# A streaming cross-entropy kernel: 7168 columns instead of 8192 per transfer, and a last chunk of 1024 columns

## Chip, cores, metric

One NeuronCore of a Trainium2 chip. The metric is the device time of one execution in microseconds (us); the runs of a kernel agree within about 0.3%. The span of a profile is about 2 us shorter than the device time of the same run.

## The reference

```python
def reference(pred, target):          # both float32, 8192 x 8192
    eps = 1e-7
    pred = np.clip(pred, eps, 1 - eps)
    return -(target * np.log(pred) + (1 - target) * np.log(1 - pred))
```

The targets are 0 or 1, so the kernel computes -ln|pred + target - 1|: one logarithm per element.

## The kernel before

It views each matrix as 64 chunks of 128 partitions x 8192 columns. A chunk is one contiguous piece of 4 MiB, so neighbouring partitions' rows lie 32 KiB apart. Four slots of a ring hold chunks in flight; target is converted to bf16 by its transfer. Each chunk takes `clip` (DVE), `front` (subtract-add on DVE, then Abs and Ln on ACT), `back` (multiply by -1, DVE) and a store.

```python
W = 8192
SLOTS = 4
# ... (rings, slot)
    def load(k):
        queue = nc.sync if k == 0 else nc.gpsimd
        queue.dma_start(out=slot(ring_p, k), in_=pred_c[k])
        nc.gpsimd.dma_start(out=slot(ring_t, k), in_=target_c[k])

    def store(k, off=0, w=W):
        queue = nc.sync if k >= n - 2 else nc.gpsimd
        queue.dma_start(out=out_c[k, :, off : off + w], in_=slot(ring_p, k, off, w))
# ... (clip, front, back; the first loads; clip(0), front(0))
        for k in range(1, n - 1):
            clip(k)
            front(k)
            back(k - 1)
            store(k - 1)
            if k >= 2 and k - 2 + SLOTS < n:
                load(k - 2 + SLOTS)
        clip(n - 1)
        back(n - 2)
        store(n - 2)
        # ... the last chunk in quarters, with two half stores
```

## Time and profile before

| | before |
|---|---|
| device time, first three runs | 1868.99 us (1868.84 to 1870.61) |
| busiest engine | DVE, 60% of the span |
| DMA | full in all 40 slices, 431 GB/s of HBM traffic |
| period of the loop | 29.05 us per chunk |
| transfers | 193 |

Read it from the bytes: 805.31 MB move in any version.

### The profile page before, as it was taken

To read this page: it belongs to the slowest core of one execution; us is meant where nothing else is said; L and a number is where in the kernel's file an instruction comes from. 1 tells how busy PE (TensorE), PEld (TensorE's weight loads), DVE (VectorE), ACT (ScalarE), POOL (GpSimd) and SP (SyncE) were. 2 spreads that over 40 slices of the span, in tenths; PEclk is the share of its full clock that TensorE was granted. 3 is DMA by queue.
4 is the path that set the end of the run, shared out by engine and by line. 5 is a ranking of instruction groups with operands and counts; after the bars stand their busy time and mean duration, and the time that the engine had idled before them with its cause. 6 is when DMAs were issued, how large, how long until landed. Compare 5 with 4: busy or idle time off the path is not lost.

```text
span 1867.5 us, 759 instructions
## 1 busy us (share of the span) xinstructions
DVE 1117.6 (60%) x199; ACT 902.4 (48%) x136; POOL 110.6 (6%) x193
## 2 busy tenths in 40 slices
DVE  4846564656656656566565665656656566566664
ACT  3643635546355364553644535445354463544635
POOL 0210000000000000000000000000000000000000
DMA  9999999999999999999999999999999999999999
GB/s 326 337 378 350 352 376 344 377 352 351 381 345 374 358 344 386 343 371 362 344 388 341 366 368 344 386 344 360 370 344 384 348 355 375 345 378 355 348 381 344
DMA packets 27797, 671.14 MB, mean 359 GB/s; under 512 B 3088, under 2 KB 3088, under 8 KB 3088
## 3 DMA queue, kind: packets, MB, share of 16 engines
q0 software_dynamic: 27216, 658.52, 98.9%
q1 hardware_dynamic: 576, 12.58, 1.6%
q14 instruction: 5, 0.04, 0.0%
HBM read 536.87 MB, written 268.44 MB: 431 GB/s over the span
## 4 chain that ended last, share of the span: by engine, by line
issue 87%; DMA 6%; POOL 5%; DVE 1%; ACT 1%; POOLq 0%; DVEq 0%; PEldq 0%
DMA ring_t<-in_target_dram 4%; DMA out_dram<-ring_p 2%; POOL ring_t L59 2%; POOL out_dram L63 2%; POOL ring_p L58 1%; DVE ring_p L73 1%; ACT ring_p L77 0%; ACT ring_p L76 0%; DVE ring_p L81 0%; POOLq L58 0%; DVEq L73 0%; PEldq L138 0%; POOLq L63 0%
## 5 line engine op out<-in xcount | busy, mean ns | idle before, releaser
L76 ACT ACTIVATE ring_p<-ring_p 128x8192 f32<-128x8192 f32 (+1 forms) x67 | 450.6, 6725 | 949.5 <-DVE ring_p L73 949.5
L73 DVE SCALAR_TENSOR_TENSOR ring_p<-ring_t,ring_p 128x8192 f32<-128x8192 bf16 (+1 forms) x67 | 556.6, 8309 | 326.0 <-DMA ring_t<-in_target_dram 326.0
L67 DVE TENSOR_SCALAR ring_p<-ring_p 128x8192 f32<-128x8192 f32 x64 | 283.3, 4426 | 406.6 <-DMA ring_p<-in_pred_dram 406.6
L77 ACT ACTIVATE ring_p<-ring_p 128x8192 f32<-128x8192 f32 (+1 forms) x67 | 450.6, 6725 | 2.1
L81 DVE TENSOR_SCALAR ring_p<-ring_p 128x8192 f32<-128x8192 f32 (+1 forms) x67 | 283.3, 4228 | 5.0 <-ACT ring_p L77 5.0
L63 POOL DMA_DIRECT2D out_dram<-ring_p x62 | 40.8, 659 | 1691.8 <-DVE ring_p L81 1661.8
L58 POOL DMA_DIRECT2D ring_p<-in_pred_dram x63 | 36.1, 574 | 18.7 <-DMA out_dram<-ring_p 18.4
L59 POOL DMA_DIRECT2D ring_t<-in_target_dram x64 | 35.3, 552 | 0.8 <-PEq L138 0.8
L87 ACT ACT_TABLE_LOAD x1 | 1.3, 1283 | 0.7 <-PEq L127 0.7
L86 DVE MEMSET warm<- 1x8 f32 x1 | 0.1, 65 | 0.8 <-PEq L127 0.8
L87 ACT ACTIVATE warm<-warm 1x8 f32<-1x8 f32 x1 | 0.2, 208 | 0.0
L127 POOL MEMSET const-float32-0.0<- 128x1 f32 x1 | 0.1, 98 | 0.2 <-issue 0.2
L127 POOL MEMSET const-bfloat16-1.0<- 128x1 bf16 x1 | 0.1, 101 | 0.0
L127 POOL MEMSET const-float32-1.0<- 128x1 f32 x1 | 0.1, 98 | 0.0
L127 POOL MEMSET const-uint8-127<- 128x1 uint8 x1 | 0.1, 98 | 0.0
## 6 DMA issues: line engine op xcount, KB each, us to landing
ring_p<-in_pred_dram POOLq DMA_DIRECT2D x63, 4096.0 KB, 34.5
out_dram<-ring_p POOLq DMA_DIRECT2D x62, 4096.0 KB, 25.3
ring_t<-in_target_dram POOLq DMA_DIRECT2D x64, 2048.0 KB, 43.7
ring_p<-in_pred_dram SPq DMA_DIRECT2D x1, 4096.0 KB, 19.5
out_dram<-ring_p SPq DMA_DIRECT2D x1, 4096.0 KB, 20.2
out_dram<-ring_p SPq DMA_DIRECT2D x2, 2048.0 KB, 11.6
```

The costliest lines, as they stand in the source:

```text
L58: queue.dma_start(out=slot(ring_p, k), in_=pred_c[k])
L59: nc.gpsimd.dma_start(out=slot(ring_t, k), in_=target_c[k])
L63: queue.dma_start(out=out_c[k, :, off : off + w], in_=slot(ring_p, k, off, w))
L67: nc.vector.tensor_scalar(out=p, in0=p, scalar1=EPS, scalar2=1 - EPS, op0=Alu.max, op1=Alu.min)
L73: nc.vector.scalar_tensor_tensor(out=p, in0=t, scalar=1.0, in1=p, op0=Alu.subtract, op1=Alu.add)
L76: nc.scalar.activation(out=p, in_=p, func=Act.Abs)
L77: nc.scalar.activation(out=p, in_=p, func=Act.Ln)
L81: nc.vector.tensor_scalar(out=p, in0=p, scalar1=-1.0, scalar2=None, op0=Alu.mult)
L86: nc.vector.memset(warm, 1.0)
L87: nc.scalar.activation(out=warm, in_=warm, func=Act.Ln)
L127: nc = _bacc.Bacc("TRN2", target_bir_lowering=False, num_devices=1)
```

## The change

The intent: a row pitch that is an odd number of 4 KiB (28 KiB instead of 32), and a tail in which only a small chunk comes last, behind two full stores, in place of a last chunk cut in quarters.

```diff
-W = 8192
+WIDE = 7 * 1024
 SLOTS = 4
+
+def plan(total):
+    n, last = divmod(total, WIDE)
+    assert 0 < last < WIDE
+    return [WIDE] * n + [last]
 ... (views and ring slots follow the widths)
-        clip(0)
-        front(0)
-        for k in range(1, n - 1):
+        for k in range(n):
             clip(k)
+            if k == n - 1:
+                back(k - 1)
+                store(k - 1)
             front(k)
-            back(k - 1)
-            store(k - 1)
+            if 0 < k < n - 1:
+                back(k - 1)
+                store(k - 1)
             if k >= 2 and k - 2 + SLOTS < n:
                 load(k - 2 + SLOTS)
-        clip(n - 1)
-        back(n - 2)
-        store(n - 2)
-        ... (quarters of the last chunk)
+        back(n - 1)
+        store(n - 1)
```

More of the change, by code (lines that the diff above doesn't have):

```diff
@@ L38, with chunk, slot @@
     R, C = pred.shape
-    n = R * C // (P * W)
-    assert n * P * W == R * C and n > SLOTS
-    def chunks(ap):
-        return ap.rearrange("r c -> (r c)").rearrange("(k p w) -> k p w", p=P, w=W)
-    pred_c, target_c, out_c = chunks(pred), chunks(target), chunks(out)
+    widths = plan(R * C // P)
+    n = len(widths)
+    cols = [sum(widths[:k]) for k in range(n)]
+    def chunk(ap, k):
+        flat = ap.rearrange("r c -> (r c)")
+        return flat[cols[k] * P : (cols[k] + widths[k]) * P].rearrange("(p w) -> p w", p=P)
     pool = ctx.enter_context(tc.tile_pool(name="rings", bufs=1))
-    ring_p = pool.tile([P, SLOTS * W], fp32, name="ring_p", tag="ring_p")
-    ring_t = pool.tile([P, SLOTS * W], bf16, name="ring_t", tag="ring_t")
+    ring_p = pool.tile([P, SLOTS * WIDE], fp32, name="ring_p", tag="ring_p")
+    ring_t = pool.tile([P, SLOTS * WIDE], bf16, name="ring_t", tag="ring_t")
     warm = pool.tile([1, 8], fp32, name="warm", tag="warm")
-    def slot(ring, k, off=0, w=W):
-        c = k % SLOTS * W + off
+    def slot(ring, k, off=0, w=None):
+        w = w or widths[k]
+        c = k % SLOTS * WIDE + off
         return ring[:, c : c + w]
@@ L57, in load, with store, clip @@
         queue = nc.sync if k == 0 else nc.gpsimd
-        queue.dma_start(out=slot(ring_p, k), in_=pred_c[k])
-        nc.gpsimd.dma_start(out=slot(ring_t, k), in_=target_c[k])
-    def store(k, off=0, w=W):
+        queue.dma_start(out=slot(ring_p, k), in_=chunk(pred, k))
+        nc.gpsimd.dma_start(out=slot(ring_t, k), in_=chunk(target, k))
+    def store(k, off=0, w=None):
+        w = w or widths[k]
         queue = nc.sync if k >= n - 2 else nc.gpsimd
-        queue.dma_start(out=out_c[k, :, off : off + w], in_=slot(ring_p, k, off, w))
-    def clip(k, off=0, w=W):
+        queue.dma_start(out=chunk(out, k)[:, off : off + w], in_=slot(ring_p, k, off, w))
+    def clip(k, off=0, w=None):
         p = slot(ring_p, k, off, w)
@@ L69, in clip, with front @@
         )
-    def front(k, off=0, w=W):
+    def front(k, off=0, w=None):
         p, t = slot(ring_p, k, off, w), slot(ring_t, k, off, w)
@@ L77, in front, with back @@
         nc.scalar.activation(out=p, in_=p, func=Act.Ln)
-    def back(k, off=0, w=W):
+    def back(k, off=0, w=None):
         p = slot(ring_p, k, off, w)
@@ L87 @@
         nc.scalar.activation(out=warm, in_=warm, func=Act.Ln)
-        clip(0)
-        front(0)
-        for k in range(1, n - 1):
+        for k in range(n):
             clip(k)
+            if k == n - 1:
+                back(k - 1)
+                store(k - 1)
             front(k)
-            back(k - 1)
-            store(k - 1)
+            if 0 < k < n - 1:
+                back(k - 1)
+                store(k - 1)
             if k >= 2 and k - 2 + SLOTS < n:
                 load(k - 2 + SLOTS)
-        clip(n - 1)
-        back(n - 2)
-        store(n - 2)
-        q = W // 4
-        front(n - 1, 0, q)
-        front(n - 1, q, q)
-        front(n - 1, 2 * q, q)
-        back(n - 1, 0, q)
-        back(n - 1, q, q)
-        store(n - 1, 0, 2 * q)
-        front(n - 1, 3 * q, q)
-        back(n - 1, 2 * q, q)
-        back(n - 1, 3 * q, q)
-        store(n - 1, 2 * q, 2 * q)
+        back(n - 1)
+        store(n - 1)
 _INS = ['pred', 'target']
```

## The prediction

> **What bounds the kernel now.** I read the page first: the busy table, the slices, the queue table and the HBM line. Then I read the issues with their landings, the waits, the groups by shape, the chain of waits in order of time, and last the timeline and the windows of the final 60 us.
>
> From the page:
>
> ```profile
> DVE 1117.6 (60%) x199; ACT 902.4 (48%) x136; POOL 110.6 (6%) x193
> DMA  9999999999999999999999999999999999999999
> ...
> q0 software_dynamic: 27216, 658.52, 98.9%
> ...
> HBM read 536.87 MB, written 268.44 MB: 431 GB/s over the span
> ```
>
> No engine is busy more than 60% of the span, while the DMA row is full in all 40 slices. The traffic is 536.87 + 268.44 = 805.31 MB, and the diff does not change it: each element of pred and target is still read once and each result written once. At 431 GB/s over the whole span the kernel moves data nearly as fast as it ever will.
>
> The issues with their landings give the unit cost:
>
> ```profile
> ring_p<-in_pred_dram POOLq DMA_DIRECT2D x63, 4096.0 KB, 34.5
> out_dram<-ring_p POOLq DMA_DIRECT2D x62, 4096.0 KB, 25.3
> ring_t<-in_target_dram POOLq DMA_DIRECT2D x64, 2048.0 KB, 43.7
> ```
>
> Per chunk the POOL queue gets a store, a pred load and a target load, one behind the other. They land 9.2 us apart and are issued 0.53 us apart, so each takes about 9.7 us. The target load reads 4 MiB of HBM although it writes only 2 MiB, because it converts to bf16. So the HBM side counts.
>
> The chain of waits in order of time shows the period of the loop (start, length, what):
>
> ```profile
> 135.42 27.61 issue
> 164.64 27.90 issue
> 194.15 28.24 issue
> 224.00 28.17 issue
> ...
> 428.98 27.49 issue
> 458.08 27.43 issue
> ...
> 1765.14 27.39 issue
> ```
>
> "Issue" here is POOL with nothing to do until the next store is ready. From 428.98 to 1765.14 there are 46 periods: 29.05 us each, and 12.583 MB per period is 433.2 GB/s. From 135.42 to 428.98 there are 10 periods of 29.36 us, so the early part lost about 3.1 us.
>
> The timeline of the end (start, length, engine):
>
> ```profile
> 1808.26 8.69 DVE L73 SCALAR_TENSOR_TENSOR ring_p<-ring_t,ring_p 128x8192 f32<-128x8192 bf16 x1 [5.29 <-DMA ring_t<-in_target_dram]
> 1816.87 4.42 DVE L81 TENSOR_SCALAR ring_p<-ring_p 128x8192 f32<-128x8192 f32 x1
> 1816.99 7.03 ACT L76 ACTIVATE ring_p<-ring_p 128x8192 f32<-128x8192 f32 x1 [14.95 <-DVE ring_p L73]
> 1821.59 0.54 POOL L63 DMA_DIRECT2D out_dram<-ring_p  x1 [27.45 <-DVE ring_p L81]
> 1824.05 7.03 ACT L77 ACTIVATE ring_p<-ring_p 128x8192 f32<-128x8192 f32 x1
> ...
> 1836.40 19.96 SPq L63 DMA_DIRECT2D out_dram<-ring_p  x3
> ```
>
> and the window of its stores:
>
> ```profile
> 1837.00:1856.00 19.00, 13.71 (x8) 14.95 (x8) 0.00 (x0) 1.00 0.99 426
> ```
>
> After the last target load has landed (1837.2) only stores remain, and the DMA share is still 0.99: the tail runs without a hole. Check: when the target of the chunk before the last lands, at 1808.26, six DMAs are left. 6 x 9.68 = 58.1 gives 1866.4, and the last data packet in the trace ends at 1866.0.
>
> **What the Trainium skill says.** (1) "DMA: Bandwidth & Descriptors", section "Where 436 GB/s comes from": 16 ports x 32 B x 850 MHz = 435.2 GB/s. The steady loop's 433.2 agrees and leaves 0.5%. (2) "HBM Reference", section "Specifications (TRN2)": a core's share is about 358 GB/s, but a core alone gets about 425. The trace shows 431, so this is the case of a core alone. (3) The DMA page, section "Latency and other measured facts": row pitches of large powers of two slow a copy, and 4 KiB of padding restored it. The pitches tabulated are 512 KiB and more; here it is 32 KiB and the steady loop is at full rate, so the trace shows no such loss outside perhaps the early 3.1 us. (4) Same page, "Specifications": first byte about 1 us after a GpSimd-issued DMA and 0.6 us after a Sync one. Here SP issued at 0.74 and the first packet started at 1.75: 1.0 us.
>
> **The change, part by part.** The diff changes the shape of the transfers: 64 chunks of 8192 columns become 73 of 7168 and one of 1024 (524288 = 73 x 7168 + 1024). I call them k = 0 to 73; s, p, t are store, pred load, target load.
>
> 1. *Steady loop.* 28.91 us of each 29.05 are 12.583 MB at 435.2 GB/s, so a DMA costs 0.045 us beyond its bytes. A wide DMA is 3.670 MB: 8.43 + 0.045 = 8.48 us. A small one is 0.524 MB: 1.25 us. There were 193 DMAs and there will be 222. Cost: 29 x 0.045 = **+1.3 us**.
>
> 2. *Does the queue stay fed?* From the landing of t(k), the DVE does 8.69 + 4.42 us before s(k-1) and the next loads are issued: 13.33 us (1808.26 to 1821.59). Three DMAs, 29.05 us, are queued then, so 15.7 us remain. After: the groups by shape have two widths, 8192 and 2048, so I interpolate.
>
> ```profile
> L73 DVE SCALAR_TENSOR_TENSOR ring_p<-ring_t,ring_p 128x8192 f32<-128x8192 bf16 x63 | 547.6, 8692 | 325.0 <-DMA ring_t<-in_target_dram 325.0
> L81 DVE TENSOR_SCALAR ring_p<-ring_p 128x8192 f32<-128x8192 f32 x63 | 278.4, 4419 | 0.0
> ...
> L73 DVE SCALAR_TENSOR_TENSOR ring_p<-ring_t,ring_p 128x2048 f32<-128x2048 bf16 x4 | 9.0, 2285 | 1.0 <-DMA ring_t<-in_target_dram 1.0
> ...
> L81 DVE TENSOR_SCALAR ring_p<-ring_p 128x2048 f32<-128x2048 f32 x4 | 4.9, 1224 | 5.0 <-ACT ring_p L77 5.0
> ```
>
> At 7168: subtract-add 7.62, multiply 3.89, and the ACT pass 6.18 (from 7032 and about 1900 ns). The issue comes 13.33 - 1.07 - 0.53 = 11.73 us after the landing, with 25.43 queued: 13.7 us remain. Fed. Cost: **0**.
>
> 3. *The tail.* Here the order decides. Let X be the landing of t72. Behind it are queued s70, p73 and t73, but the last chunk is now tiny: 8.48 + 1.25 + 1.25 = 10.98 us instead of 29. s71 is issued only at X + 11.73 and its packets start about 1.2 us later (an estimate from the skill's 1 us and POOL's 0.54 us issue), at X + 12.9. **First hole: about 1.9 us.** s71 ends at X + 21.4. Meanwhile s72: DVE ready at X + 7.66, two ACT passes (6.20 + 6.18) to X + 20.04, multiply to X + 23.95, Sync's issue and 1.0 us to X + 25.0. **Second hole: about 3.6 us.** s72 runs to X + 33.5. Chunk 73 needs 1.22 + 2 x 1.05 + 0.69, so it is ready at about X + 28 and s73 follows without a hole to X + 34.7. Together **+5.5 us**. Before, one full chunk of loads covered this chain; now the last compute chain of a wide chunk (16.3 us from subtract-add done to stored) has just 10.98 us of loads and one store above it. Splitting the last chunk in quarters, which is removed, had no cost on the path.
>
> 4. *Pitch of 28 KiB.* The steady loop can't be faster than 435.2. What the pitch can give is the early 3.1 us. The slow packets there (up to 1.9 us where 1.23 is normal) are the last target packets in front of a store, and vanish after 400 us. Whether the cause is the pitch the profile does not say. I take half: **-1.5 us**.
>
> Sum: 1868.99 + 1.3 + 0 + 5.5 - 1.5 = 1874.3; I predict **1874 us**.
>
> **The rivals.**
> (a) *The pitch matters more than I think*, all 3.1 us come back, and the holes are half as long: 1868.99 + 1.3 - 3.1 + 2.8 = 1870. For: the early slow periods exist. Against: 46 equal periods at 433.2 GB/s.
> (b) *The early slow packets don't fade*, because with the new pitch the 16 engines stay in step: a slow period cost up to 0.8 us (194.15 to 224.00 is 29.85), at half of that 73 x 0.4 = 29 us more, 1905. For: the fading is unexplained. Against: nothing in the smaller pitch is known to hold engines together.
> (c) *A short tail is a gain*: a smaller last store ends the kernel sooner. It would, if the end waited for compute; 1866.4 worked out against 1866.0 seen says that it waits for bytes. At most the holes vanish: 1868.8.
> (d) *DVE becomes the bound.* Its total hardly moves: 73 x (2 x 3.89 + 7.62) + 2.6 = 1127 us of 1870. No.
>
> **Range and chances.** Floor: 805.31 MB at 435.2 is 1850.4, plus the 1.75 before the first packet, 222 x 0.045 = 10 and 3 for the end and launch: 1865, if neither holes nor early loss remain. So over 2% faster (under 1832) is out of reach: 0.01. Over 2% slower (above 1906) needs (b) at its worst: 0.03. Range 1868 to 1882: below it every doubt would have to go one way, above it rival (b) by a third.
>
> **What would show it.** Step 1: a period of 25.43 us in the chain of waits. Step 2: the waits of POOL's stores for DVE unchanged in kind, the DMA row full up to the last slice. Step 3: in the windows of the last 35 us, the DMA share clearly under 0.99, with the last wide store issued by Sync about 24 us after the last wide target landed. Step 4: early periods of the same length as late ones. Wrong would be: a steady period under 25.3 or over 25.8, no holes in the last 35 us, or an end that comes sooner than the bytes allow.

## The result

| | before | after |
|---|---|---|
| device time, median | 1869.2 us (4 runs) | 1876.22 us (4 runs, 1875.68 to 1877.61) |
| ratio | | 1.0037 (1.002 to 1.0055) |
| period of the loop | 29.05 us | 25.44 us |
| last data packet ends | 1866.0 us | 1874.6 us |
| all 16 DMA engines idle in the tail | 0 | 5.6 us |

A ratio here is the mean time of one kernel's fast runs over the mean of the other's fast runs of the same rounds, so it is not quite the ratio of the medians. The change costs 7.0 us by the medians, 0.4%. The profiled run of the changed kernel (1877.61) is the slowest of its four, so its end lies a little later than the medians say.

From the page of the changed kernel, the DMA row and the HBM line:

```profile
DMA  9999999999999999999999999999999999999997
...
HBM read 536.87 MB, written 268.44 MB: 429 GB/s over the span
```

The bytes are the same. What is new is the 7 in the last slice, where the kernel before had a 9. (The GB/s of a window or slice counts a target packet by the bf16 bytes that it writes, so it is lower than the HBM line: 360 against 431.)

The chain of waits of the changed kernel (start, length, what):

```profile
120.82 24.43 issue
146.85 23.81 issue
...
428.38 24.04 issue
...
1776.83 23.81 issue
```

From 428.38 to 1776.83 there are 53 periods, so 25.44 us each; 11.01 MB per period is 432.8 GB/s. The steady loop neither gained nor lost. From 120.82 to 428.38 there are 12 periods of 25.63.

The timeline of the changed kernel's end:

```profile
1839.79 7.62 DVE L82 SCALAR_TENSOR_TENSOR ring_p<-ring_t,ring_p 128x7168 f32<-128x7168 bf16 x1 [4.63 <-DMA ring_t<-in_target_dram]
1847.34 3.88 DVE L90 TENSOR_SCALAR ring_p<-ring_p 128x7168 f32<-128x7168 f32 x1
...
1851.52 0.54 POOL L72 DMA_DIRECT2D out_dram<-ring_p  x1 [23.85 <-DVE ring_p L90]
1853.66 6.18 ACT L86 ACTIVATE ring_p<-ring_p 128x7168 f32<-128x7168 f32 x1
1859.87 3.89 DVE L90 TENSOR_SCALAR ring_p<-ring_p 128x7168 f32<-128x7168 f32 x1 [8.04 <-ACT ring_p L86]
...
1863.79 4.37 SPq L72 DMA_DIRECT2D out_dram<-ring_p  x2
```

and windows over it (the next-to-last number is the DMA share, the last GB/s):

```profile
1839.80:1845.80 6.00, 6.00 (x1) 0.00 (x0) 0.00 (x0) 1.00 0.94 361
1845.80:1853.00 7.20, 6.03 (x3) 5.55 (x1) 0.54 (x1) 1.00 0.24 91
1853.00:1861.00 8.00, 1.13 (x1) 6.81 (x2) 0.00 (x0) 1.00 0.94 401
1861.00:1865.00 4.00, 3.90 (x2) 0.07 (x1) 0.00 (x0) 1.00 0.27 115
```

X, the landing of the last wide target, is 1839.79 (taken as the start of the subtract-add that waits for it). The lines show two troughs in the DMA share, 0.24 and 0.27, each ended by a store that had to wait for DVE. In the trace's packet records no engine moves data from 1850.34 to 1852.62 and from 1861.33 to 1864.64: holes of 2.3 and 3.3 us. They count only moments in which even the slowest engine is idle. The faster ones lose more: all 16 are still moving data at 1845.4, but only about 4 at 1846.2, while the slowest goes on to 1850.3. Counted over all engines, the idle time in the last 45 us of transfers is 9.8 us per engine here and 2.6 in the kernel before.

### The profile page after: what moved, and what is told of

It reads as the page before. It is cut to its first block, busy times and chain, and to the rows that moved or that the text cites. A ratio compares the mean times of both kernels' runs of the same rounds, so it can differ in the third digit from the quotient of the medians.

```text
span 1875.8 us, 858 instructions
## 1 busy us (share of the span) xinstructions
DVE 1120.9 (60%) x223; ACT 905.6 (48%) x150; POOL 124.9 (7%) x223
## 4 chain that ended last, share of the span: by engine, by line
issue 87%; POOL 5%; DMA 5%; DVE 1%; ACT 1%; POOLq 0%; DVEq 0%; PEldq 0%
DMA ring_t<-in_target_dram 3%; POOL ring_t L67 2%; POOL out_dram L72 2%; DMA out_dram<-ring_p 2%; POOL ring_p L66 2%; DVE ring_p L82 1%; ACT ring_p L85 0%; ACT ring_p L86 0%; DVE ring_p L90 0%; POOLq L66 0%; DVEq L82 0%; POOLq L72 0%; PEldq L136 0%
## 5 line engine op out<-in xcount | busy, mean ns | idle before, releaser
L85 ACT ACTIVATE ring_p<-ring_p 128x7168 f32<-128x7168 f32 x74 | 452.1, 6109 | 958.4 <-DVE ring_p L82 958.4
L82 DVE SCALAR_TENSOR_TENSOR ring_p<-ring_t,ring_p 128x7168 f32<-128x7168 bf16 x74 | 557.9, 7539 | 331.8 <-DMA ring_t<-in_target_dram 331.7
L76 DVE TENSOR_SCALAR ring_p<-ring_p 128x7168 f32<-128x7168 f32 x74 | 285.0, 3851 | 404.0 <-DMA ring_p<-in_pred_dram 404.0
L86 ACT ACTIVATE ring_p<-ring_p 128x7168 f32<-128x7168 f32 x74 | 452.1, 6109 | 2.4
L90 DVE TENSOR_SCALAR ring_p<-ring_p 128x7168 f32<-128x7168 f32 x74 | 284.4, 3843 | 10.3 <-ACT ring_p L86 10.3
L72 POOL DMA_DIRECT2D out_dram<-ring_p x72 | 45.1, 626 | 1709.3 <-DVE ring_p L90 1682.9
L66 POOL DMA_DIRECT2D ring_p<-in_pred_dram x73 | 41.0, 562 | 16.6 <-DMA out_dram<-ring_p 16.3
L67 POOL DMA_DIRECT2D ring_t<-in_target_dram x74 | 40.3, 545 | 1.0 <-PEq L136 0.8
```

The costliest lines, as they stand in the source:

```text
L66: queue.dma_start(out=slot(ring_p, k), in_=chunk(pred, k))
L67: nc.gpsimd.dma_start(out=slot(ring_t, k), in_=chunk(target, k))
L72: queue.dma_start(out=chunk(out, k)[:, off : off + w], in_=slot(ring_p, k, off, w))
L76: nc.vector.tensor_scalar(out=p, in0=p, scalar1=EPS, scalar2=1 - EPS, op0=Alu.max, op1=Alu.min)
L82: nc.vector.scalar_tensor_tensor(out=p, in0=t, scalar=1.0, in1=p, op0=Alu.subtract, op1=Alu.add)
L85: nc.scalar.activation(out=p, in_=p, func=Act.Abs)
```

## The experiments

My theory: the loss is the two holes (5.6 us) and 29 more transfers (1.3 us), while the pitch does nothing. The rival: the narrower runs or their pitch are what costs, in the loop or early on. A finer question is whether each hole is a cost by itself, or whether one chain of compute sets the end. The runs of the first four experiments share a chip and the runs of before (median 1869.38, though two of these nine took 1873.5 and 1873.8), and so do the runs of the last four (1869.77). Differences of 2 us or less are therefore near the noise, and the traces have to carry them.

### 28 KiB runs, but the small chunk first and the old tail

```diff
-    return [WIDE] * n + [last]
+    return [last] + [WIDE] * n
 ... (loop and quartered tail of the kernel before, quarters of 1792 columns)
```

> The 28 KiB runs and the 222 transfers of the changed kernel stay, but the 1024-column chunk comes first and the end is the quartered tail of the kernel before. Tail theory (the loss is two holes in the last 35 us, 5.6 us, plus 0.045 us for each added transfer): 1870.5, so 1.3 us over before, and no time in the last 60 us in which all 16 DMA engines are idle. Pitch theory (28 KiB runs themselves are slower, or the early slow packets last longer): 1875 or more, with the tail full.

Measured: 1871.91 us (1871.29 to 1875.89), ratio 1.0014 (0.9999 to 1.0029). The window of the tail, and no moment with all engines idle in the packet records:

```profile
1837.00:1862.00 25.00, 13.71 (x8) 14.95 (x8) 0.00 (x0) 1.00 0.99 427
```

```profile
1837.00:1862.00 25.00, 17.54 (x10) 14.13 (x9) 0.00 (x0) 1.00 0.98 401
```

The first line is the kernel before, the second this run: the tail is as full. (The lower GB/s of the second line is the last target load, which lands at 1843.3 here and counts by its bf16 bytes.) So the 28 KiB runs with the old tail are some 4 us faster than with the new one (1876.09 on the same chip, for the changed kernel with one multiply moved, two experiments below). The two half stores make the transfers 223, not 222. The time is 1.4 above what I expected; one of the five runs (1875.89) stands apart, and this excess I did not resolve. The packets show no loss by the narrower runs: by the median a pred or store packet of 32 KiB took 1.213 us in the kernel before and one of 28 KiB 1.062 us here, 27.0 GB/s per engine in both.

### 32 KiB pitch with the new tail

```diff
-WIDE = 7 * 1024
+WIDE = 8 * 1024
-    assert 0 < last < WIDE
-    return [WIDE] * n + [last]
+    assert last == 0
+    return [WIDE] * (n - 1) + [WIDE - 1024, 1024]
```

> The 32 KiB pitch of the kernel before (63 chunks of 8192, one of 7168, one of 1024) with the changed kernel's loop and tail. Tail theory: with X the landing of the last wide target, queued behind it 9.68 + 1.25 + 1.25 us, the second-last wide store comes at X + 12.3 and the last at X + 24.0: holes of about 1.2 and 1.8 us, so about 3 us over before, 1872. Pitch theory: as before, 1869.

Measured: 1873.38 us (1872.32 to 1875.18), ratio 1.0018 (1.0006 to 1.0031): 3.4 us by the ratio, 4.0 by the medians. Windows:

```profile
1843.00:1851.00 8.00, 6.56 (x3) 6.31 (x2) 0.54 (x1) 1.00 0.27 102
...
1860.00:1862.00 2.00, 2.00 (x2) 0.00 (x0) 0.00 (x0) 1.00 0.54 229
```

The holes in the packet records are 1.6 and 1.6 us (expected 1.2 and 1.8). With the old pitch, and only two more transfers than before, the new tail loses time by itself. They are smaller than in the changed kernel, as the sums in the expectation have it: the two stores over the chain are a full 9.68 us each here instead of 8.48.

### The multiply of chunk 71 moved ahead

```diff
-            if k == n - 1:
+            if k >= n - 2:
                 back(k - 1)
                 store(k - 1)
             front(k)
-            if 0 < k < n - 1:
+            if 0 < k < n - 2:
```

> The changed kernel, with the multiply and store of chunk 71 moved ahead of the subtract-add of chunk 72 (DVE is idle there, waiting for t72), so that s71 is issued about 12 us sooner. If the end is set by the chain subtract-add, two ACT passes, multiply, store of chunk 72, the first hole closes, the second grows by the same, and the time is that of the changed kernel, 1876 within 0.5. If each hole is a cost by itself: 2 us less, 1874.

Measured: 1876.09 us (1876.01 to 1876.24), ratio 1.0031 (1.0018 to 1.0044), the time of the changed kernel. The timeline and a window of this run:

```profile
1837.85 0.54 POOL L72 DMA_DIRECT2D out_dram<-ring_p  x1 [11.54 <-DVE ring_p L90]
1838.43 7.62 DVE L82 SCALAR_TENSOR_TENSOR ring_p<-ring_t,ring_p 128x7168 f32<-128x7168 bf16 x1 [0.88 <-DMA ring_t<-in_target_dram]
```

```profile
1854.00:1864.00 10.00, 5.03 (x2) 4.91 (x2) 0.00 (x0) 1.00 0.16 69
```

The store of chunk 71 is issued before X, and the first hole is gone. In its place there is a single hole of 5.8 us (1857.44 to 1863.27). Two holes of 5.6 became one of 5.8, and the end did not move: the last packet ends 34.83 us after X in the changed kernel and in this run. In the experiment above this one, whose last wide chunk has the same 7168 columns behind wider stores, it is 34.83 us too. So the end is set by one chain: last wide target, subtract-add, Abs, Ln, multiply, store. Closing a gap that lies beside the chain was worth nothing.

### The last wide chunk in two halves

```diff
 ... (the loop ends at chunk 72 and leaves its front to these lines)
+        h = WIDE // 2
+        front(n - 2, 0, h)
+        front(n - 2, h, h)
+        clip(n - 1)
+        back(n - 2, 0, h)
+        store(n - 2, 0, h)
+        front(n - 1)
+        back(n - 2, h, h)
+        store(n - 2, h, h)
         back(n - 1)
         store(n - 1)
```

on top of the run before.

> As the run before, and chunk 72 is computed and stored in two halves, so that its first half is stored at about X + 12.4 and its second at about X + 18.5, both before s71 is through at X + 19.5. Tail theory: no hole is left, 5.6 us come back: about 1870.5, and the last packet ends 29.2 us after X instead of 34.8. If the tail is not the cause: 1875 or more.

Measured: 1870.44 us (1869.49 to 1871.11), ratio 1.0001 (0.9988 to 1.0013). Windows:

```profile
1850.00:1854.00 4.00, 2.82 (x2) 3.97 (x2) 0.00 (x0) 1.00 0.94 405
1854.00:1861.00 7.00, 2.72 (x2) 3.93 (x3) 0.00 (x0) 1.00 0.92 391
1861.00:1864.00 3.00, 0.00 (x0) 0.00 (x0) 0.00 (x0) 1.00 0.99 414
```

No hole is left in the packet records, and 1876.09 - 1870.44 = 5.65 us came back, against 5.6 expected. Pitch, loads and loop are those of the changed kernel; only the last wide chunk's compute and store are cut in two. The last packet ends at 1868.1, 28.8 us after X (1839.29) where 29.2 was expected. This settles the tail.

### A pitch of 2 MiB

```diff
-        return ap.rearrange("r c -> (r c)").rearrange("(k p w) -> k p w", p=P, w=W)
+        return ap.rearrange("r c -> (r c)").rearrange("(p k w) -> k p w", p=P, w=W)
```

in the kernel before.

> The kernel before with one line changed: each partition owns one contiguous stretch of 524288 columns, so rows of a chunk are 2 MiB apart instead of 32 KiB; sizes, counts and order of transfers stay. It asks whether pitch matters on this kernel at all. If pitches of large powers of two alias in HBM as the skill's measured 2 MiB row has it (164 GB/s against 214): about 1.3 times, 2440. If 32 KiB runs hide it: 1869.

Measured: 2049.43 us (2046.22 to 2051.14), ratio 1.0959 (1.0944 to 1.0974). Both numbers that I wrote down were wrong: the loss is there, but it is 180 us and not 570. (The 164 and 214 GB/s are from "DMA: Bandwidth & Descriptors" of the Trainium skill, section "Latency and other measured facts", for copies between HBM tensors.) The same window of the kernel before, then of this run:

```profile
1000.00:1200.00 200.00, 118.86 (x22) 98.44 (x14) 11.18 (x21) 1.00 1.01 360
```

```profile
1000.00:1200.00 200.00, 107.60 (x20) 84.38 (x12) 9.59 (x18) 1.00 1.00 332
```

The DMA share is full in both, and the rate is 8% lower: some packets take longer (a target packet in this window 1.38 us on average against 1.23, with the median over the whole run at 1.23 in both). A loss by this layout therefore shows in the kernel where it exists. At 32 KiB no such loss is seen: the steady loop runs at 433.2 GB/s. The edit also makes a chunk 128 separate rows instead of one contiguous piece, and no run separates that from the pitch.

### 4096 columns: twice the transfers

```diff
-W = 8192
+W = 4096
```

in the kernel before.

> The kernel before at 4096 columns: 16 KiB pitch, 128 chunks, 385 transfers instead of 193, tail as before. It measures the cost of a transfer by itself: 192 x 0.045 = 8.6 more, 1878. If a transfer costs nothing beyond its bytes: 1869; if the shorter backlog lets the queue run dry, clearly above 1880 with holes in the DMA row.

Measured: 1881.24 us (1880.85 to 1885.67), ratio 1.0067 (1.0053 to 1.008): by the medians 11.5 us for 192 more transfers, 0.060 each. In its chain of waits:

```profile
1098.48 13.00 issue
...
1799.62 13.01 issue
```

there are 48 periods of 14.607 us between these two. 6.291 MB at 435.2 GB/s are 14.456, which leaves 0.050 per transfer. The third case, a queue that runs dry, did not happen although the time is above 1880: the DMA row is full in all 40 slices, and the packet records show no moment with all engines idle before the end. The term of 0.045 was of the right size; the rest of the 11.5 is in longer packets here and there (4.2 us per engine beyond their usual time, against 2.0 in the kernel before).

### 6144 columns: an even number of 4 KiB

```diff
-WIDE = 7 * 1024
+WIDE = 6 * 1024
```

in the run with the small chunk first.

> 6144 columns, so a pitch of 24 KiB, an even number of 4 KiB, with the small chunk first and the quartered tail, as in the run of 28 KiB with the small chunk first (1871.9 measured). 259 transfers against 222: if only the number of transfers counts, 37 x 0.045 = 1.7 above that run, 1873.6. If the odd number of 4 KiB is worth anything, clearly more than that, 1876 or above.

Measured: 1871.58 us (1871.18 to 1872.04), ratio 1.001 (0.9997 to 1.0022). A pitch of 24 KiB is no slower than one of 28 KiB (1871.91, on the other chip; by the ratios 1.001 against 1.0014), in spite of 36 more transfers (259 against 223; the expectation's 222 left out the second half store). The odd number of 4 KiB is worth nothing that these runs can see. The run is 2 us faster than expected, so the count of transfers explains differences of this size only to within about 2 us.

### All stores from Sync

```diff
-        queue = nc.sync if k >= n - 2 else nc.gpsimd
+        queue = nc.sync
```

in the kernel before.

> The kernel before with all stores issued from Sync instead of GpSimd, so that they go through another ring and mix with the loads packet by packet. The early loss (slow target packets just in front of a store, some 2 to 3 us in the first 400 us) stands in both kernels. If it comes from all engines switching from loads to stores at once, it vanishes: about 1866.5, better than both kernels. If not: 1869, or slower if stores delayed by competing loads let the ring run dry.

Measured: 1876.44 us (1873.38 to 1877.76), ratio 1.0033 (1.002 to 1.0046). I hoped for a version that beats both and got a slower one. Its timeline and a window:

```profile
1849.76 6.70 DVE L73 SCALAR_TENSOR_TENSOR ring_p<-ring_t,ring_p 128x2048 f32<-128x2048 bf16 x3 [10.30 <-DMA ring_t<-in_target_dram]
```

```profile
1854.00:1860.00 6.00, 3.88 (x4) 5.94 (x4) 0.00 (x0) 1.00 0.16 67
```

The subtract-add of the last chunk starts at 1849.8 instead of 1837.3, as the stores now pass the queued loads and the last target lands later (the median time from a target's issue to its landing is 49.1 us against 43.7). Little is then left to move while the last chunk is computed, and the packet records show holes of 4.0 and 2.4 us. It is the same fault as in the changed kernel, made in another way. The slow packets between 100 and 400 us did go (0.75 us per engine before, 0.00 here), but the earlier ones, from 20 to 100 us, stayed (0.54 before, 0.60 here), and the last packet ends at 1874.4; less the 6.4 us of holes that is 1868.0, not below before's 1866.0.

No version ran faster than the kernel before, and nothing in these runs points to one.

## Why the prediction was right, and where it was off

It said 1874, in 1868 to 1882, and 1876.22 was measured.

- **Step 1, right.** The period is 25.44 us (25.43 predicted). The cost of a transfer, 0.045, was measured as 0.050 in a steady loop and 0.060 over a whole run of 4096 columns; for 29 transfers 1.3 to 1.7 us.
- **Step 2, right.** The DMA row is full up to the last slice. POOL's store s71 came 1851.52 - 1839.79 = 11.73 us after X, the predicted 11.73.
- **Step 3, right.** Sync's store came at X + 24.00 and its first packet at X + 24.85 (predicted 25.0); the holes were 2.3 and 3.3 us (predicted 1.9 and 3.6), together 5.6 against 5.5. The first hole opened at X + 10.55 instead of X + 10.98, and POOL's packets started 1.10 us after its issue. (The prediction has about 1.2; the two terms that it names, 1 and 0.54, would be 1.54.) The last packet ended at X + 34.8 (predicted 34.7). Splitting the last wide chunk gave back 5.65. What I presented as two costs is one chain, as the run with the early multiply showed; the sum is the same. That the sum fits better than its two parts is therefore no luck: it is the chain, 25.0 us predicted and 24.85 measured, less the bytes queued over it.
- **Step 4, wrong.** "I take half: -1.5 us" was the term that failed. The pitch gave back nothing that can be seen. Counting what packets took beyond 30 ns over the median of their size, the loss per engine is 1.98 us before and 2.01 after. The early periods lost 12 x (25.63 - 25.44) = 2.3 us where before lost 3.1 over ten, but more went before them, between 20 and 100 us (0.75 per engine against 0.54). Without this term the sum is 1868.99 + 1.3 + 5.5 = 1875.8.
- **The ceiling, right as a number.** The prediction compared 435.2 GB/s ("DMA: Bandwidth & Descriptors" of the Trainium skill, section "Where 436 GB/s comes from", a ceiling of the SBUF ports) with bytes of HBM. On the SBUF side the same loop moved only 10.486 MB per 29.05 us, 361 GB/s, because target lands as bf16. A target packet, which reads 32 KiB and writes 16, took 1.23 us, about as long as a pred packet (1.21). So counting HBM bytes was right here, but these runs do not show that the SBUF ports are what limits.
- **Rival (a)**, all 3.1 us back and half the holes, did not happen: nothing came back and the holes were 5.6 us. **Rival (b)**, slow packets that don't fade, did not happen. **Rival (c)**, a gain from a short tail, is refuted by the 32 KiB pitch with the new tail. **Rival (d)**, DVE as the bound, did not happen: DVE was busy for 60% of the span (1120.9 us).

What causes the slow early packets stays open. They are there with pitches of 24, 28 and 32 KiB, and mixing the stores in removed only the later ones.

## What to carry to other kernels

In a kernel bound by DMA, the end is a race between the bytes still queued when the last large load lands and the compute chain from that load to its store. Add both up: here 10.98 us of queued transfers and 8.48 us of one more store, 19.5 together, stood over a chain of 25.0 us from the landing to the first packet of the last wide store, and the difference of 5.5 was lost. So keep large loads queued behind the second-last chunk, or cut the compute of the last large chunk finely, and check with the DMA share in narrow windows; a hole beside the chain may be closed without gain. The first two are measured here: 1871.91 us with the old tail and 1870.44 with the cut chunk, against 1876.09.

## What the Trainium skill lacked or had wrong

- "DMA: Bandwidth & Descriptors", "Latency and other measured facts", the pitch row: it starts at 512 KiB and gives, for copies between HBM tensors, 164 GB/s at 2 MiB and 214 for a padded pitch. Here a 2 MiB pitch cost 9.6% of the time, with 32 KiB rows, and with nearly all loads and stores through GpSimd's queue. It has no small pitches: 24, 28 and 32 KiB ran alike (1871.6, 1871.9 and 1869.4 us with full tails and 259, 223 and 193 transfers), so an odd multiple of 4 KiB had nothing to give at this size.
- Same page, "Anatomy of one DMA": it gives a fixed cost of about 2 us per DMA. Behind a full queue one more transfer cost 0.045 to 0.060 us here; the page has no number per transfer for that case.
- No page says how far the 16 DMA engines drift apart within one queue. At the end of the kernel before they finished between 1862.3 and 1866.0 us. In the changed kernel about 12 of the 16 had run out of work by 1846.2, while the slowest had some until 1850.3; a hole counted by the slowest engine is longer for the others.
- "HBM Reference" gives about 425 GB/s for a core alone. The steady loop held 433.2, reads and writes together.
